# RWKV-7 time mixing: both Gram products of three key groups as one with 128 moved columns, receptances before the inverse, a new step order

## The chip, the core and the metric

One NeuronCore of a Trainium2 chip runs the kernel; the other cores of the chip are not used. The metric is the device time of one launch in microseconds (us). The engines have short names here as in the profile: PE is TensorE (matrix products; PEld is its loading of the stationary operand), DVE is VectorE, ACT is ScalarE, POOL is GpSimd, SP is SyncE, which issues the DMAs. PE writes into PSUM, which has eight banks of 128 x 512 float32; DVE and ACT read it.

## What is computed

A decoder trunk of two layers on 256 tokens of width 1024, in float32. The change lies wholly in the time mixing of the first layer, a delta rule with data-dependent decay over 16 heads of 64:

```python
r = xr @ w_rkv[0]; k = xk @ w_rkv[1]; v = xv @ w_rkv[2]
...
def step(S, inp):
    r_t, w_t, k_t, v_t, kk_t, b_t = inp
    sa = jnp.einsum('bhij,bhj->bhi', S, -kk_t)
    S = (S * w_t[:, :, None, :] + sa[..., None] * b_t[:, :, None, :]
         + v_t[..., None] * k_t[:, :, None, :])
    y = jnp.einsum('bhij,bhj->bhi', S, r_t)
    return S, y
...
_, y = lax.scan(step, S0, xs)          # 256 steps
# group norm per head, a bonus term, a gate, then
return (y * g) @ w_o
```

Around it stand the four gated FFNs (width 2816), the RMS norms and, in the second layer, sliding-window attention.

## The kernel before

The scan over 256 tokens is not run step by step. The tokens are cut into chunks of 64, and within a chunk the rule is solved as a triangular system: strictly causal 64x64 **Gram products** of the removal keys (`kk`) with the scaled keys and `b` vectors give the matrices `GS` and `GX`; a 32x32 **inverse** of their diagonal blocks runs on DVE (`invert`, step `inv`), `merge` (steps `m0`, `m1`) joins two 32x32 blocks to a 64x64 inverse `W`; a **chain** (`c00`, `c01` for the first pair of chunks of all heads, `c10`, `c11` for the second; the last digit is one half of the heads) multiplies with `GS`, `W`, `GX` in turn and copies between them on ACT; `state` (`st`) carries the state from the first pair to the second; `rows` (`y0`, `y1`) multiplies the causal Gram products with the **receptances** (`GR`, `GY`) to the output, and group norm (`gn0`, `gn1`), gate, transposition (`yt`) and output projection (`o0`, `o1`) follow.

Features go through in four **groups** p = 0 to 3 of 256 features (4 heads). For each group `k_mm` (`k0` to `k3`) projects the keys, `k_norm` (`n`) normalises and scales them, `r_mm` (`r`) projects the receptance, `r_fin` (`f`) scales it into AR and multiplies it with the key, `r_bo` (`b`) sums that for the bonus. `AR` holds four slots of 64 columns per head chunk: 0 and 3 are the removal keys of two chunks, 1 and 2 the receptances of the same two. Then, for each group, `g_pair` runs twice: as `s` with the removal keys (slots 0 and 3, strict mask, into GS and GX) and as `g` with the receptances (slots 1 and 2, inclusive mask, into GR and GY). One `g_pair` is 16 products with a stationary operand of 64 rows x 128 columns and 64 moved columns (line 681), two DVE evacuations with mask of 128x512 (line 684), eight more such products (line 692) and two ACT copies (line 695). The two products of a pair of heads use rows 0 to 63 and rows 64 to 127 of the array in turn (`hh`). A float32 product is recorded as two instructions, so 16 products stand as x32.

PSUM in this stage: four banks `bk` (tag of `self.bank()`), two `bc` (`self.cbank()`), two `bt` (`self.tbank()`), each in rotation.

What comes when is written out by hand: every step is a Python generator, and the string `STEPS` lists which generator goes on next. After that the order on PE, DVE and ACT is tied to the order in which the instructions were made:

```python
for nm in STEPS.split():
    next(unit[nm], None)
self.mark()
self.in_order(first, "PE", "DVE", "Activation")
```

So an instruction that waits holds up all that follows on its engine within this stage. `kw` splits the key weights (ACT, then DVE), `v01`, `v10`, `v11` project the values, `t0`, `t1` transpose keys, `w0` to `w7` split the output weights, `da` and `db` copy diagonal blocks of GS for the inverse, `bias` and `gate` prepare the group norm. Weights arrive through four rotating buffers `wr` from SP's queue. Outside this stage the kernel is the same.

Of the kernel before, what the change touches and what calls it, by code (L numbers as in the profile page):

```python
# [11 lines left out]
ALU = mybir.AluOpType  # L12
# [4 lines left out]
P = 128  # L17
# [5 lines left out]
N = 64  # L23
# [23 lines left out]
P3 = [(False, 0, 0)] * 3 + [(False, x, 2) for x in (-4, -4, -4, -3, -3, -1, -1)]  # L47
TX1, TX2 = (6, 7), (6, 7)
STEPS = """
kw kw kw k0 k0 kw k0 k0 kw kw xr k1 k1 xr kw xr xr n0 n0 kw kw n0 n0 r0 k1 k1  # L50
x1 kw kw n0 n0 k2 k2 n1 n1 n0 n1 n1 r0 f0 s0 kw s0 n1 n1 v01 k2 k2 kw kw k3 s1
s1 kw kw n2 x1 v01 n2 n2 n2 v01 k3 k3 f0 s0 n1 k3 n2 n2 n3 r3 n3 n3 s0 n3 s2 s2
v01 s1 n3 n3 r3 f3 n3 f3 s1 v01 room s3 s3 v10 v10 n2 b0 da r1 r1 db b0 t1 v10 v11 t0
v00 t0 t1 inv v10 s2 dc s2 inv v11 v11 t1 t1 t0 t0 inv r2 r2 f1 b3 s3 v11 inv s3 v10 inv
v11 inv g1 inv inv inv b3 m0 m0 c01 m1 m1 f1 b1 b1 g1 c00 m1 f2 w3 f2 m1 w0 w0 c01 g0
g0 b2 b2 w4 gate gate0 bias0 w4 bias0 c00 w3 gate0 gate0 m0 bias1 c01 m0 c01 gate0 g1 g1 c00 c00 g0 g0 c00
c00 c01 c00 c01 c10 c01 c01 c11 g2 g2 c00 st w1 g3 st g3 c11 w2 g3 g3 c10 w2 g2 g2 y0 c11
y0 w1 c10 c10 c10 bias1 c11 gn0 c10 gn0 c11 gn0 gn0 gn0 gn0 gn0 gn0 gn0 c11 c10 gate1 gate1 c11 gate1 w5 gn0
y1 w6 y1 c10 gn0 gn0 yt0 c10 gate1 w6 c11 w5 yt0 yt0 c11 y1 gn1 gn1 yt0 yt0 gn1 gn1 o0 o0 yt0 gn1
gn1 gn1 gn1 gn1 gn1 gn1 w7 o0 o0 o0 gn1 w7 o0 o0 yt1 yt1 yt1 yt1 o0 o1 o1 yt1 yt1 o1 o1 o1  # L60
o1 o1 o1
"""


class Trunk:
# [507 lines left out]
    def tm_core(self):  # L573
        nc, a, DC = self.nc, self.a, self.DC
        mm = nc.tensor.matmul
        TT, STT = nc.vector.tensor_tensor, nc.vector.scalar_tensor_tensor
# [6 lines left out]
        for j in range(2):  # L583
            t = self.pp.tile([P, D], F32, name=f"gain{self.uid()}", tag="gain", bufs=3)
# [36 lines left out]
        kw = lambda tag, shape, bufs: self.pools["kw"].tile(shape, F32R, name=f"{tag}_{self.uid()}", tag=tag, bufs=bufs)  # L621
# [10 lines left out]
        BH = self.tl("el", [P, 2, KT, P], tag="BH")  # L632
        Di = pk("Di", [P, KT, 4, N])
        AR = self.tl("ar", [P, 16, 4, N], tag="AR")
        BK = self.tl("ar", [P, 16, 4, N], tag="BK")
        nc.gpsimd.memset(Dp[:, :, :, 0], 1.0)
        sw, av = [], []
        for i in range(2):
            sw.append(pk("p1", [P, D], 2))
            for n in range(2):  # L640
                ns = slice(n * 512, n * 512 + 512)
                b = self.bank()
                mm(b, self.hwa[0:65, 0, toks[i]], l2[0][0:65, ns], start=True, stop=True)
                nc.scalar.activation(sw[i][:, ns], b, AF.Sigmoid)
        for p in range(4):
            b = self.bank()
# [6 lines left out]
        for n in range(2):  # L653
            for i in range(2):
                b = self.bank()
# [11 lines left out]
        masks = self.cst[:, K_MASK:K_MASK + 256].rearrange("p (e s t) -> p e s t", e=2, s=2)  # L667
        f = lambda ap: ap.rearrange("p s t -> p (s t)")
        GS = [self.tl("GS", [P, 16, 2, N], tag=f"GS{hh}") for hh in range(2)]
        GS = [(GS[hh], self.tl("GS", [P, 16, N], tag=f"GX{hh}")) for hh in range(2)]  # L670

        pair = lambda: [self.tbank() for _ in range(2)]

        def g_pair(p, lhs_rhs, dst, mask):
            bb = pair()
            for x in range(4):
                for sl in range(2):
                    for hh in range(2):
                        s = slice(hh * 64, hh * 64 + 64)
                        l, r = lhs_rhs(s, 4 * p + x, sl)  # L680
                        mm(bb[hh][:, (2 * x + sl) * N:(2 * x + sl + 1) * N], l, r, start=True, stop=True)  # L681
            yield
            for hh in range(2):
                TT(dst()[hh][0][:, 4 * p:4 * p + 4, :, :], bb[hh].rearrange("p (q s t) -> p q s t", q=4, s=2),
                   mask.unsqueeze(1).unsqueeze(1).to_broadcast([P, 4, 2, N]), op=ALU.mult)
            yield
            bb = pair()
            for x in range(4):
                for hh in range(2):
                    s = slice(hh * 64, hh * 64 + 64)  # L690
                    l, r = lhs_rhs(s, 4 * p + x, 2)
                    mm(bb[hh][:, x * N:(x + 1) * N], l, r, start=True, stop=True)  # L692
            yield
            for hh in range(2):
                nc.scalar.copy(dst()[hh][1][:, 4 * p:4 * p + 4, :], bb[hh][:, 0:256].rearrange("p (q t) -> p q t", q=4))
            yield

        def g_ops(slots):
            def at(s, q, sl):
                l = (lambda: f(BK[s, q, 0:2, :]), lambda: f(BK[s, q, 2:4, :]), lambda: BH[s, q % 2, q // 2, :])[sl]()  # L700
                return l, AR[s, q, slots[1] if sl else slots[0], :]
            return at

        kst = {}
        L = {}

        def k_split():
            for x in range(16):
                if x % 2 == 0:
                    raw = self.raw(a["w_k"][x // 2])  # L710
                w = kw("wk", [P, 2, 512], 3)
                ns = slice(x % 2 * 512, x % 2 * 512 + 512)
                self.split(w[:, 0], w[:, 1], raw[:, ns])
                kst["w", x] = w
                yield
# [63 lines left out]
        def r_mm(p):  # L779
            kst[p], todo = self.feat_raw(a["w_r"], p, L["xr"])  # L780
            for x in todo:
                x()
                yield
# [23 lines left out]
        def mix_xr():  # L807
            L["xr"] = self.tl("xt", [P, KT, T], tag="xth")
            for k in range(KT):
                self.mix_into(nc.vector, L["xr"][:, k], 0, k, slice(0, T))  # L810
                if k % 2:
                    yield

        def mix_xv1():
            L["xv1"] = vv[:, 1, :].rearrange("p (k t) -> p k t", k=KT)
            for k in range(KT):
                self.mix_into(nc.vector, L["xv1"][:, k], 3, k, toks[1])
                if k % 4 == 3:
                    yield

        def v_mm(i, n):
            acc, todo = v_half(n, L["xv1"] if i else xv)
            for x in todo:
                x()
                yield
            src = acc.rearrange("p (m hh j) -> p hh m j", hh=2, j=N)
            for e in range(2):
                rs = slice(e * 64, e * 64 + 64)
                dst = uv()[e].rearrange("p (hh m c) j -> p hh m c j", hh=2, c=2)[rs, :, n * 4:n * 4 + 4, i, :]
                nc.scalar.copy(dst, src[rs])  # L830
            yield

        def v00():
            src = v0.rearrange("p (m hh j) -> p hh m j", hh=2, j=N)
            for e in range(2):
                rs = slice(e * 64, e * 64 + 64)
                dst = uv()[e].rearrange("p (hh m c) j -> p hh m c j", hh=2, c=2)[rs, :, 0:4, 0, :]
                nc.scalar.copy(dst, src[rs])
            yield
# [9 lines left out]
        def room():  # L849
            self.close("kw", "pk")  # L850
            self.open("GR")
            self.open("Wx")
            self.open("el1")
            L["GR"] = [(self.tl("GR", [P, 16, 2, N], tag=f"GR{hh}"), self.tl("GR", [P, 16, N], tag=f"GY{hh}"))
                       for hh in range(2)]
            L["Dg"] = sp("c", [P, 32, 32])
            yield

        def dg(q0, q1):
            for x, (s0, sl, c0) in enumerate(((64, 0, 0), (96, 0, 32), (0, 1, 0), (32, 1, 32))):  # L860
                for hh in range(2):
                    (nc.vector.tensor_copy if q0 and hh else nc.scalar.copy)(
                        L["Dg"][s0:s0 + 32, hh * 16 + q0:hh * 16 + q1, :], GS[hh][0][s0:s0 + 32, q0:q1, sl, c0:c0 + 32])
            yield
# [33 lines left out]
        def decays():  # L898
            nc.scalar.copy(DC, Dp[:, :, :, N])
            yield  # L900
# [216 lines left out]
        def out_proj(i):  # L1117
# [3 lines left out]
            for k in range(KT):  # L1121
# [5 lines left out]

        unit = {"xr": mix_xr(), "x1": mix_xv1(), "room": room(), "da": dg(0, 12), "db": dg(12, 16), "inv": invert(),
                "dc": decays(), "kw": k_split(), "v00": v00(), "v01": v_mm(0, 1), "v10": v_mm(1, 0), "v11": v_mm(1, 1),
                "st": state(), "gate": gates()}  # L1130
        for p in range(4):
            unit.update({f"k{p}": k_mm(p), f"n{p}": k_norm(p), f"r{p}": r_mm(p), f"f{p}": r_fin(p), f"b{p}": r_bo(p),
                         f"s{p}": g_pair(p, g_ops((0, 3)), lambda: GS, masks[:, 0, 0]),
                         f"g{p}": g_pair(p, g_ops((1, 2)), GRs, masks[:, 0, 1])})
        for i in range(2):
            unit.update({f"m{i}": merge(i), f"t{i}": bk_turn(i), f"y{i}": rows(i), f"bias{i}": gn_bias(i),
                         f"gate{i}": gn_gate(i), f"gn{i}": normed(i), f"yt{i}": turned(i), f"o{i}": out_proj(i),
                         f"c{i}0": chain(i, 0), f"c{i}1": chain(i, 1)})
# [316 lines left out]
```

## Time and profile before

| | |
|---|---|
| median of 3 runs | 1082.4 us (1079.42 to 1084.34) |
| the profiled execution | 1087.76 us, of which the span of its instructions is 1086.0 us |
| PE busy, share of the span | 97% |
| DVE, ACT busy | 64%, 52% |
| DMA, mean | 169 GB/s |
| the stage of the change | from 235.0 us (first key product) to 418.0 us (end of the output projection) |

The profiled execution is one more run of the same kernel, 5.4 us above the median of the others. Busy time of PE includes the latency of products that overlap, so a busy PE can still run slowly: the granted clock says how fast it ran.

### The profile page before, as it was taken

Reading aid. Unit: us, or ns where it says so; the run is one execution under the profiler, and the core shown is the slowest. Engines: PE = TensorE matmul, PEld = TensorE weight load, DVE = VectorE, ACT = ScalarE, POOL = GpSimd, SP = SyncE. Lnnn points to the kernel's source line nnn. Section 1 sums busy time; section 2 is a strip of 40 time slices with the busy share of each in tenths; the row PEclk is TensorE's granted clock in tenths of the full one; section 3 lists DMA queues with packets and bytes.
Section 4 is the critical chain, followed back from the end, with each engine's and each line's share of the span. In section 5 each row is a group of like instructions: output and inputs, shape, how many; then the busy total and the mean of one; then the engine's idle time right before and its main releaser. Section 6 shows DMA issues by size and latency. Waiting matters only on the chain.

```text
span 1086.0 us, 16426 instructions
## 1 busy us (share of the span) xinstructions
PE 1058.1 (97%) x6408; PEld 878.3 (81%) x6408; DVE 693.2 (64%) x1108; ACT 566.4 (52%) x1014; POOL 32.7 (3%) x44
## 2 busy tenths in 40 slices
PE   7999999999999999999999999999999899999997
PEld 5888888698778987888888788888887568888885
DVE  6766654647696498855655686565656767665652
ACT  6654644464415346655554765555636665655541
POOL 0000000000000000000000100000012200000000
PEclk9999999999996899999999999999999999999999
DMA  8768664224363134866664286676532535765621
GB/s 290 237 193 290 197 191 136 74 101 137 123 187 95 45 118 156 272 202 207 191 193 137 97 271 204 188 249 194 180 110 98 175 97 195 214 211 187 184 76 39
DMA packets 52670, 183.06 MB, mean 169 GB/s; under 512 B 5744, under 2 KB 6000, under 8 KB 52464
## 3 DMA queue, kind: packets, MB, share of 16 engines
q1 hardware_dynamic: 52304, 181.49, 52.3%
q8 instruction: 50, 0.82, 0.3%
q10 hardware_dynamic: 288, 0.52, 0.1%
q14 instruction: 28, 0.23, 0.1%
HBM read 180.94 MB, written 1.05 MB: 168 GB/s over the span
## 4 chain that ended last, share of the span: by engine, by line
PE 90%; ACT 3%; DVE 2%; DMA 2%; issue 2%; POOL 1%; SPq 0%; DVEq 0%; POOLq 0%; ACTq 0%
PE bk L213 35%; PE bt L348 13%; PE bk L348 13%; PE bt L349 6%; PE bk L349 6%; PE bk L557 3%; PE bk L603 2%; PE bt L681 2%; PE bk L567 1%; PE bt L692 1%; PE bc L962 1%; PE bk L1013 1%; PE bt L295 1%; DMA wr<-in_w_in_dram 1%; ACT g2k L1236 1%
## 5 line engine op out<-in xcount | busy, mean ns | idle before, releaser
L187 DVE TENSOR_TENSOR W<-wr,W 128x1024 fp32r<-128x1024 f32 x275 | 335.8, 1226 | 192.7 <-ACT W L181 191.3
L181 ACT CAST W<-wr 128x1024 fp32r<-128x1024 f32 x280 | 292.8, 1051 | 200.8 <-issue 107.5
L213 PE MATMUL bk<-W,g2k 128*128 128x512 f32 x1056 | 251.5, 394 | 0.0
L213 PEld LDWEIGHTS bk<-W,g2k 128*128 128x128 f32 x1056 | 195.5, 188 | 45.1
L348 PE MATMUL bt<-xtl,W 128*128 128x512 f32 x296 | 105.9, 397 | 0.3 <-DVE xtl L336 0.3
L348 PE MATMUL bt<-xth,W 128*128 128x512 f32 x296 | 105.9, 396 | 0.0
L348 PE MATMUL bk<-xtl,W 128*128 128x512 f32 x296 | 105.7, 396 | 0.0
L348 PE MATMUL bk<-xth,W 128*128 128x512 f32 x296 | 105.7, 396 | 0.0
L349 PE MATMUL bt<-xtl,W 128*128 128x256 f32 x296 | 83.1, 281 | 0.0
L349 PE MATMUL bk<-xth,W 128*128 128x256 f32 x296 | 83.1, 281 | 0.0
L349 PE MATMUL bt<-xth,W 128*128 128x256 f32 x296 | 83.1, 281 | 0.0
L349 PE MATMUL bk<-xtl,W 128*128 128x256 f32 x296 | 83.0, 280 | 0.0
L348 PEld LDWEIGHTS bt<-xtl,W 128*128 128x128 f32 x296 | 55.6, 188 | 14.0 <-DVE xtl L336 0.7
L348 PEld LDWEIGHTS bk<-xth,W 128*128 128x128 f32 x296 | 55.6, 188 | 13.3
L348 PEld LDWEIGHTS bt<-xth,W 128*128 128x128 f32 x296 | 55.5, 188 | 13.3
L348 PEld LDWEIGHTS bk<-xtl,W 128*128 128x128 f32 x296 | 55.6, 188 | 13.0
L213 PE MATMUL bk<-W,xtl 128*128 128x512 f32 x216 | 55.9, 404 | 1.5 <-ACT xtl L300 0.7
L349 PEld LDWEIGHTS bk<-xtl,W 128*128 128x128 f32 x296 | 55.8, 188 | 1.3
L349 PEld LDWEIGHTS bt<-xtl,W 128*128 128x128 f32 x296 | 55.8, 189 | 0.1
L349 PEld LDWEIGHTS bk<-xth,W 128*128 128x128 f32 x296 | 55.8, 189 | 0.0
L349 PEld LDWEIGHTS bt<-xth,W 128*128 128x128 f32 x296 | 55.7, 189 | 0.1
L213 PE MATMUL bk<-W,xth 128*128 128x512 f32 x216 | 53.5, 394 | 0.0
(260 smaller groups left out, 1429.0 us busy)
## 6 DMA issues: line engine op xcount, KB each, us to landing
wr<-in_w_in_dram SPq DMA_DIRECT2D x148, 512.0 KB, 4.0
wr<-in_w_out_dram SPq DMA_DIRECT2D x88, 512.0 KB, 3.6
wr<-in_w_in_lead_dram SPq DMA_DIRECT2D x28, 512.0 KB, 4.0
wr<-in_w_v_dram SPq DMA_DIRECT2D x16, 512.0 KB, 3.7
gain<-in_rows_dram SPq DMA_DIRECT2D x13, 512.0 KB, 4.6
wr<-in_w_k_dram SPq DMA_DIRECT2D x8, 512.0 KB, 4.2
wr<-in_w_r_dram SPq DMA_DIRECT2D x8, 512.0 KB, 4.2
wr<-in_w_o_dram SPq DMA_DIRECT2D x8, 512.0 KB, 3.8
```

What stands on the lines that cost most here:

```text
L181: self.follow(nc.scalar.copy(w[:, 0, :], raw), 0)
L187: self.follow(nc.vector.tensor_tensor(w[:, 1, :], raw, w[:, 0, :], op=ALU.subtract), 1)
L213: mm = lambda *x, **y: self.nc.tensor.matmul(*x, **y, **kw)
L295: t = self.nc.tensor.transpose(b[:, k * P:(k + 1) * P], xn[:, c:c + P], self.ident)
L348: mm(banks[j], hi[:, c0:c0 + P], xt[c][:, :, k4, :], start=(k == 0), stop=False)
L349: use[0] = mm(banks[j][:, 0:T], lo[:, c0:c0 + P], xt[c][:, 0, k4, :], start=False, stop=(k == KT - 1))
L557: self.nc.tensor.matmul(b[:, j * T:(j + 1) * T], ws[k // 4][:, c0:c0 + P], xf[:, k, :], start=(k == 0), stop=(k == KT - 1))
L567: nc.tensor.matmul(bs[j], l[:, k, j * P:(j + 1) * P], x[:, k, sl], start=(k == 0 and not e), stop=(k == KT - 1 and e == 1))
L603: mm(acc, x[:, 2 * k2 + k, :], w[:, k, :], start=(k2 + k == 0), stop=(k2 + k == 4))
L681: mm(bb[hh][:, (2 * x + sl) * N:(2 * x + sl + 1) * N], l, r, start=True, stop=True)
L692: mm(bb[hh][:, x * N:(x + 1) * N], l, r, start=True, stop=True)
L962: mm(b[r, m * N:(m + 1) * N], W[r, v - hh * 16, :], XV[r, v, :], start=True, stop=True)
```

## The change

A new generator `g_both(p)` makes the products of `s` and `g` of one group together: for each stationary operand the two neighbouring slots of AR (a removal key and a receptance) are moved at once, 128 columns in place of 64. It has three parts of eight products each, in a pair of `bk`, `bt` and `bc` banks; the first two are evacuated by four DVE instructions of 128x256 each (the half for GS with the strict mask, the half for GR; both read the mask of their kind), the third by four ACT copies of 128x256. Groups 0, 1 and 2 use it (steps `q0`, `q1`, `q2`); group 3 keeps `s3` and `g3`. Since a `q` needs the receptances of its group, `r0`, `r1`, `r2` now come before the inverse, and `STEPS` is written anew from end to end; `r3` and most of the value products stand within the inverse.

```diff
@@ STEPS (one line of each; the table is replaced whole)
-v11 inv g1 inv inv inv b3 m0 m0 c01 m1 m1 f1 b1 b1 g1 c00 m1 f2 w3 f2 m1 w0 w0 c01 g0
+g3 inv m1 c01 m1 m0 m0 g3 c00 m1 m1 f3 b3 b3 w0 gate0 bias0 bias0 c01 q2 q2 q2 c00 g3 gate0 gate0
...
+        def g_both(p):
+            for sl, new in enumerate((lambda: [self.bank() for _ in range(2)], pair,
+                                      lambda: [self.cbank() for _ in range(2)])):
+                bb = new()
+                for x in range(4):
+                    q = 4 * p + x
+                    for hh in range(2):
+                        s = slice(hh * 64, hh * 64 + 64)
+                        l = BH[s, q % 2, q // 2, :] if sl == 2 else f(BK[s, q, 2 * sl:2 * sl + 2, :])
+                        mm(bb[hh][:, x * P:(x + 1) * P], l, f(AR[s, q, 2 * min(sl, 1):2 * min(sl, 1) + 2, :]),
+                           start=True, stop=True)
+                yield
+                qs = slice(4 * p, 4 * p + 4)
+                for kind in range(2):
+                    for hh in range(2):
+                        G = (GS, L["GR"])[kind][hh]
+                        b = bb[hh].rearrange("p (q s t) -> p q s t", q=4, s=2)[:, :, kind if sl == 0 else 1 - kind, :]
+                        if sl == 2:
+                            nc.scalar.copy(G[1][:, qs, :], b)
+                        else:
+                            TT(G[0][:, qs, sl, :], b, masks[:, 0, kind].unsqueeze(1).to_broadcast([P, 4, N]),
+                               op=ALU.mult)
+                    yield
...
+        for p in (0, 1, 2):
+            unit[f"q{p}"] = g_both(p)
```

Where the new order tells most, in rows of the two programs as they are built (line, operation, output and inputs, shape; lines behind `g_both` are 24 to 26 higher in the changed kernel).

DVE, just ahead of the inverse, before: GS is the masked Gram product, `c` the diagonal blocks, `a` and `b` the inverse's matrices.

```order
L792 SCALAR_TENSOR_TENSOR km_1938<-bk_2468,cols,km_1938 128x256 x2
L684 TENSOR_TENSOR GS_316_2006<-bt_2571,cst 128x512
L684 TENSOR_TENSOR GS_317_2007<-bt_2572,cst 128x512
L774 TENSOR_TENSOR BH_1939<-BK_1942,Dp_1937 128x2x2x128
L862 COPY c_2570<-GS_317_2007 32x128 x4
L875 STREAM_TRANSPOSE a_2668<-c_2570 128x1024
L880 TENSOR_TENSOR c_2673<-a_2668,b_2669 128x31
```

The same place in the changed kernel (L727 is `g_both`'s evacuation, L886, L798 and L899 are the old L862, L774 and L875):

```order
L727 TENSOR_TENSOR GR_382_2481<-bk_2585,cst 128x4x64
L727 TENSOR_TENSOR GR_384_2483<-bk_2586,cst 128x4x64
L727 TENSOR_TENSOR GS_316_2006<-bt_2609,cst 128x4x64
L727 TENSOR_TENSOR GS_317_2007<-bt_2610,cst 128x4x64
L727 TENSOR_TENSOR GR_382_2481<-bt_2609,cst 128x4x64
L727 TENSOR_TENSOR GR_384_2483<-bt_2610,cst 128x4x64
L886 COPY c_2485<-GS_317_2007 32x128 x4
L798 TENSOR_TENSOR BH_1939<-BK_1942,Dp_1937 128x2x2x128
L899 STREAM_TRANSPOSE a_2678<-c_2485 128x1024
```

The last evacuations ahead of the inverse are now those of `q2`, and 24 of them stand in a row from `s3` on, where before two of `s3` stood.

PE, after the merges, before: L1049 is the gate, L916 the second half of a merge, L962 a chain's product with W, L692 a part of `g1`.

```order
L802 MATMUL bc_3063<-cst,km_1938 128x2 x4
L1049 MATMUL bk_3081<-wr_3073,sgT 128x512
L1049 MATMUL bk_3093<-wr_3073,sgT 128x512
L916 MATMUL bc_3095<-a_2870,b_2874 32x32 x32
L962 MATMUL bc_3133<-xtl_2915,W_467_2873 64x64 x8
L692 MATMUL bt_3147<-AR_1941,BH_1939 128x64
```

And now (L1073, L940, L986, L976 and L1037 are the old L1049, L916, L962, L952 and L1013):

```order
L1073 MATMUL bk_3103<-wr_2884,sgT 128x512
L986 MATMUL bc_3110<-xtl_2950,W_478_2911 64x64 x8
L940 MATMUL bc_3120<-a_2878,b_2912 32x32 x32
L976 MATMUL bk_2951<-u_2817,GX_319_2009 64x64 x8
L986 MATMUL bc_3164<-xtl_2950,W_477_2910 64x64 x8
L986 MATMUL bc_3174<-xtl_2950,W_478_2911 64x64 x8
L976 MATMUL bk_3007<-u_2817,GX_318_2008 64x64 x8
L1073 MATMUL bk_3197<-wr_2884,sgT 128x512
L986 MATMUL bc_3212<-xtl_2950,W_477_2910 64x64 x8
L1037 MATMUL bk_3222<-u_2817,GR_382_2481 64x64
```

The parts of `g0` and `g1` that stood between the chain's products are gone, the gate's four products are spread among them, and `y0` (L1037) follows straight on.

DVE, around the state between the two pairs of chunks, before: L992 and L993 scale the new state, L684 is `g2` and `g3`.

```order
L684 TENSOR_TENSOR GR_395_2566<-bt_3252,cst 128x512
L684 TENSOR_TENSOR GR_397_2568<-bt_3253,cst 128x512
L992 TENSOR_TENSOR c_3273<-bc_3274,DC 128x512
L993 TENSOR_TENSOR c_3273<-c_3273,DC 128x512
L684 TENSOR_TENSOR GR_395_2566<-bt_3311,cst 128x512
```

And now (L1016 and L1017 are the old L992 and L993; L1105 to L1118 are the group norm of the first half, L1075 and L1076 its gate):

```order
L1105 TENSOR_REDUCE gst_3272<-bk_3223 128x8
L1106 TENSOR_SCALAR gst_3272<-gst_3272 128x8
L1107 TENSOR_TENSOR xth_2891<-bk_3223,gst_3272 128x8x64
L1075 TENSOR_TENSOR gain_2886<-gain_2886,bk_3285 128x512
L1076 TENSOR_TENSOR gain_2888<-gain_2888,bk_3285 128x512
L1113 TENSOR_REDUCE gst_3272<-b_3273 128x8
L1114 TENSOR_SCALAR gst_3272<-gst_3272 128x8
L1118 TENSOR_TENSOR xth_2891<-xth_2891,gain_2890 128x8x64
L1016 TENSOR_TENSOR c_3323<-bc_3324,DC 128x512
L1017 TENSOR_TENSOR c_3323<-c_3323,DC 128x512
```

The state's two instructions now stand behind most of the first half's group norm, which itself waits for `y0`.

## Rows read from the trace of the kernel before

**Rows 1.** The profile's page: busy time of PE and DVE, and the line of the granted TensorE clock in 40 slices of the span (27.15 us each; 9 is full speed, 5 would be half).

```profile
PE 1058.1 (97%) x6408; PEld 878.3 (81%) x6408; DVE 693.2 (64%) x1108; ACT 566.4 (52%) x1014; POOL 32.7 (3%) x44
...
PEclk9999999999996899999999999999999999999999
```

**Rows 2.** The sums by stretch over the stage: length, busy time (and instructions) of PE, PEld, DVE, ACT and POOL, then the granted clock, the share of the DMA engines and GB/s.

```profile
235.00:297.80 62.80, 62.80 (x490) 54.14 (x489) 41.93 (x83) 31.08 (x66) 1.11 (x2) 1.00 0.39 127
297.80:330.30 32.50, 32.50 (x186) 23.92 (x185) 29.30 (x70) 7.94 (x18) 0.00 (x0) 1.00 0.61 182
330.30:335.90 5.60, 5.07 (x188) 4.79 (x188) 2.67 (x5) 3.40 (x9) 0.00 (x0) 1.00 0.20 78
335.90:360.30 24.40, 24.40 (x290) 20.98 (x284) 13.55 (x18) 9.44 (x17) 0.00 (x0) 0.51 0.20 66
360.30:373.50 13.20, 13.20 (x312) 12.63 (x312) 6.47 (x9) 4.18 (x7) 0.00 (x0) 1.00 0.02 5
373.50:376.90 3.40, 3.40 (x54) 3.28 (x54) 0.89 (x1) 1.71 (x4) 0.00 (x0) 0.50 0.80 288
```

**Rows 3.** The chain of work that ended last, in order of time (start, length, what): a pass of the 16 Gram products and one of the eight at full clock, 32 receptance instructions of 256 moved columns (one group's `r`), two of the four parts of a value product, and two turns of keys (`t`).

```profile
292.86 1.93 PE bt L681 x32
...
299.21 7.01 PE bk L557 x32
...
306.66 3.44 PE bk L603 x8
...
312.25 1.04 PE bt L692 x16
...
316.92 0.87 PE bt L974 x8
```

**Rows 4.** PE in order of time in the attention stage (start, length of the group, line, shape of the stationary operand, what is written): products of 64 rows x 128 columns with 128 moved columns, four on one half of the rows and then four on the other half, and what starts next.

```profile
823.55 2.82 PE L1222 MATMUL bk<-kT,qT 64*128 64x128 f32 x32 [0.19 <-DVE qT L1199]
826.29 0.73 PE L213 MATMUL bk<-W,xtl 128*128 128x512 f32 x2
```

**Rows 5.** DVE in order of time: evacuations from PSUM of two widths, the copy of diagonal blocks, the start and the end of the inverse.

```profile
294.10 0.87 DVE L792 SCALAR_TENSOR_TENSOR km<-bk,cols,km 128x256 f32<-128x256 f32 x2
294.89 1.27 DVE L684 TENSOR_TENSOR GS<-bt,cst 128x512 f32<-128x512 f32 x2
296.08 0.68 DVE L774 TENSOR_TENSOR BH<-BK,Dp 128x512 f32<-128x512 f32 x1
296.80 0.92 DVE L862 COPY c<-GS 32x128 f32<-32x128 f32 x4
297.81 1.95 DVE L875 STREAM_TRANSPOSE a<-c 128x1024 f32<-128x1024 f32 x1
...
327.68 0.88 DVE L895 TENSOR_SCALAR W<-a,cst 128x512 f32<-128x512 f32 x2
```

**Rows 6.** The chain of work that ended last, from the end of the inverse on: the first half of a merge, twice (L907), the chain's first products (L937), a bonus sum (L802), and two pieces of the low-clock stretch.

```profile
330.37 1.13 PE bc L907 x64
331.50 1.08 PE bk L937 x32
332.58 1.00 PE bc L907 x56
334.43 0.98 PE bc L802 x8
335.41 1.46 PE bk L937 x32
...
338.71 3.61 PE bt L681 x32
...
357.18 3.22 PE bk L952 x32
```

**Rows 7.** The same view around the state (L988) and after it: the chain's product with the state (L945), `g3`'s first pass (L681), `y0` (L1013), two products with W (L962), two with GX (L952), two of the gate (L1049) and the state's part of `y1` (L1003).

```profile
365.68 2.06 PE bc L988 x64
367.74 1.93 PE bt L681 x32
369.67 1.08 PE bk L945 x32
...
374.88 4.80 PE bk L1013 x96
379.68 2.00 PE bc L962 x32
381.68 2.14 PE bk L952 x32
383.82 1.92 PE bk L1049 x4
385.74 1.84 PE bk L1003 x62
```

**Rows 8.** DVE in order of time: the state's two instructions, and the first instruction of each half of the heads in the group norm `gn0` (three instructions each).

```profile
367.78 0.69 DVE L992 TENSOR_TENSOR c<-bc,DC 128x512 f32<-128x512 f32 x1 [0.78 <-PE bc L988]
368.50 0.69 DVE L993 TENSOR_TENSOR c<-c,DC 128x512 f32<-128x512 f32 x1
...
378.78 0.69 DVE L1081 TENSOR_REDUCE gst<-bk 128x8 f32<-128x512 f32 x1 [4.39 <-PE bk L1013]
...
380.32 0.68 DVE L1081 TENSOR_REDUCE gst<-bk 128x8 f32<-128x512 f32 x1
```

More of the change, by code (lines that the diff above doesn't have):

```diff
@@ L49 @@
 STEPS = """
[L50 to L54, printed above, removed]
-v11 inv g1 inv inv inv b3 m0 m0 c01 m1 m1 f1 b1 b1 g1 c00 m1 f2 w3 f2 m1 w0 w0 c01 g0
[L56 to L61, printed above, removed]
+kw k0 kw k0 kw k0 kw kw k0 x1 xr kw k1 kw kw k1 k1 dc xr kw kw xr xr k1 k2 k2
+kw n0 n0 n0 r0 n0 kw kw n0 n0 n1 n1 x1 r0 f0 f0 k2 k2 n1 n1 k3 r1 kw kw kw n1
+n1 n2 n2 n2 n2 r1 f1 f1 n1 f1 n0 k3 k3 n2 n2 k3 n3 n3 b1 n3 r2 b1 n3 n3 n3 n3
+room r2 f2 f2 s3 s3 q1 q1 q1 q0 q1 q1 q1 q0 q0 b0 b2 b0 q0 q0 q0 b2 q2 q2 q2 q0
+q2 q2 v11 q2 db t1 v01 v01 da q0 v01 t0 v11 t1 q0 n2 inv v01 f2 inv t0 inv inv q1 q1 s3
+s3 q1 v10 inv inv v11 t0 v11 r3 v01 inv r3 t1 v10 v00 v11 f0 t1 v10 v10 t0 f3 v10 inv w0 gate
+g3 inv m1 c01 m1 m0 m0 g3 c00 m1 m1 f3 b3 b3 w0 gate0 bias0 bias0 c01 q2 q2 q2 c00 g3 gate0 gate0
+w5 w5 c01 c01 m0 m0 c01 c01 f1 c00 c00 c01 c01 c00 bias1 gate1 c00 w3 bias1 gate1 w3 gate0 g3 c00 c00 f0
+y0 y0 gn0 gn0 gn0 w4 gate1 c11 c10 gate1 st w2 gn0 gn0 gn0 gn0 st y1 c11 gn0 c10 c11 c11 gn0 gn0 gn0
+c10 c10 gn0 c11 w4 c11 w6 w6 c10 yt0 yt0 yt0 yt0 yt0 yt0 w1 w1 w2 c10 c10 c11 y1 c10 c10 c11 c11
+y1 gn1 gn1 gn1 gn1 gn1 f2 o0 gn1 o0 w7 gn1 gn1 gn1 o0 o0 o0 o0 gn1 gn1 gn1 o0 w7 yt1 yt1 o0
+yt1 o1 o1 yt1 yt1 yt1 o1 o1 o1 o1 o1 o1
 """
```

## Prediction, made before the changed kernel was run

> **What bounds the kernel now.** I read the page first: PE is busy 97% of the span, DVE 64%, and the granted clock is full everywhere except in the 13th and 14th slice [rows 1]. The sums by stretch put that dip inside the stage of the change: PE runs at 0.51 of its clock from 335.9 to 360.3 us and at 0.50 from 373.5 to 376.9 [rows 2], 27.8 us in all. In every stretch shown but one PE has no idle time; from 330.3 to 335.9 it is busy 5.07 of 5.60 us. The reader should see two things: PE's own list of products ends last, so work taken off it counts in full, and part of that work is paid for at nearly twice its price.
>
> What does the dip cost? The same 32 Gram instructions take 1.93 us at full clock [rows 3, 7] and 3.61 in the dip [rows 6], a ratio of 1.87. By it 27.8 us of low clock do the work of 14.9: the dip costs **12.9 us**. Ahead of its fall PE worked 5.5 us on narrow pieces: 32x32 merges, 64x64 chain products and a bonus sum with two moved columns [rows 6].
>
> **The change, part by part.**
>
> *Gram products.* `s` plus `g` of one group cost 2 x (1.93 + 1.04) = 5.94 us [rows 3]. A `q` has three parts of 16 instructions with the same stationary shape and 128 moved columns. Is a part as cheap as 16 instructions with 64 columns (1.04 us), or nearly twice as dear? The attention stage has this shape: 32 instructions start between 823.55 and 826.29, 86 ns each [rows 4]. Were streaming the bound and the two halves of the array's rows never at work together, the pace of the receptances (7.01 us for 32 of 256 columns, so 110 ns for 128 columns [rows 3]) would give 3.5 us for these 32; they took 2.74. So the halves do overlap, though there they change only every eight instructions, while `q` changes at each product. Bounds of a part: 1.04 us (full overlap) and 16 x 110 ns = 1.75 us (none); by the attention row as it stands, 16 x 86 ns = 1.37. I take 1.04: the 64-column pace, 60 to 65 ns for an instruction [rows 3], is 120 to 130 for a pair, one in each half, and that already leaves room for 110 ns of streaming in each. A `q` then costs 3.1 us, and three save 3 x 2.8 = **8.5 us**; at the other end 3 x (5.94 - 5.25) = 2.1 us. All of it lies on PE's list.
>
> The Trainium skill, "TensorE: Matmul & The Clock Gate" (section "Back-to-back issue gap"), gives a lone matmul 134 cycles for 128 moved columns against some 60 for up to 64, so that joining two narrow ones would gain nothing; by that page the sum would lack the 8.5 us.
>
> *Evacuations.* Each `q` has eight DVE instructions of 128x256 in place of four of 128x512. Two of 512 columns take 1.19 us from start to the next start, two of 256 columns 0.79 [rows 5]. So a `q` asks for 3.2 us of DVE against 2.4, and 24 instructions stand in a row right ahead of the inverse: 9.5 us, or 14.3 if 256 columns cost what 512 do. What hides them is PE, which has eight parts of `q` (8.3), `s3`, two bonus sums and a value product there, as much or more. I went down the lists of PE, ACT and DVE in the new order with the durations of the trace, from the first key product at 235.0 us, and get the last evacuation near 296.5, diagonal blocks (0.9) and one BH (0.6 [rows 5]) behind it, and the inverse beginning near 298, where it began before (297.81 [rows 5]).
>
> *What is moved ahead of the merges.* All four receptances stood ahead of the first merge before too, though within the inverse. PE's list up to it loses `s0` to `s2` and `g1`'s first pass (3 x 2.97 + 1.93 = 10.8) and gains eight parts of `q` (8.3), `g3`'s first pass (1.9) and one bonus sum (0.8): 11.0. So PE reaches the merge as before, near 330. The inverse is covered: behind `q2`'s second part stand twelve value parts (1.72 each), `r3` (7.0), four turns (0.44 each), two third parts (1.04 each) and `g3`'s first pass, 33.4 us [rows 3], against some 31 us from the inverse's start to its W [rows 5]. I count nothing; bounds: 1.5 us gained (what the old kernel waited ahead of the merge, by the sum of its list), 5 us lost (below).
>
> *ACT, DMA.* ACT has as many copies as before and 52% load [rows 1]: nothing. SP issues the same loads through four `wr` buffers, `w_r` earlier and `w_v` later; I find them filled 0 to 2 us ahead of use, `v10`'s last part perhaps 0.4 us late. Nothing, with 1 us as bound.
>
> *The state.* Before, `st` ended at 367.74 and its two DVE instructions ran at once, beside `g3`'s 1.93 us on PE [rows 7, 8]: no wait. Now they stand on DVE behind most of `gn0`, which can only start when `y0` ends. On PE a gate product (0.96), two first chain products (1.08 each [rows 6]) and `st` (2.06 [rows 7]) follow `y0`: 5.2 us. On DVE 2 x 1.54 (`gn0`'s halves [rows 8]), a gate of 1.2, some 0.4 of waiting for ACT, 0.8 and 0.6 of `gn0`'s second step and the state's 1.4 make 7.5. PE's next piece, `y1`, reads that state, and all of PE's list, the chain `c10` and `c11` first, is queued behind it. A new wait of 2 to 3 us; I take **2.4**; bounds 0 (if low clock stretches PE's side beyond DVE's) and 3.1.
>
> *The low clock.* Two places behind the inverse decide. (a) From the first merge to `y0`. The first 6.2 us at full clock are narrow pieces as before, without the 0.5 us of idling [rows 2, 6]; then come two gate products of 512 columns, `q2`'s last part and a part of `g3`, chain products again, and `y0`, 4.8 us over all 128 rows [rows 7]. The clock came back before when products over all rows (L952) had run for 3.2 us, and the second time while `y0` ran [rows 2, 6, 7]. If it falls after the narrow pieces again and returns in `y0`, twelve pieces of about 1.0 us [rows 7] are paid at 1.87: 10.4 lost. (b) From the new wait to `y1`'s product over all rows: 9 us of mostly narrow pieces, where the old order had `g3`, `g2` and `y0` among them: 0 to 7.8 lost. Together 0 to 18.2; both places hold pieces of either kind, so I take the middle, 9.1. Against 12.9 before, **3.8 us** come back.
>
> **Sum.** -8.5 - 3.8 + 2.4 = -9.9 us, 1087.8 -> 1077.9 for the profiled execution. That one lay 5.4 us above the median of the runs; from the median the sum gives **1072.5 us**. A difference under 0.5% (5.4 us) this measurement can hardly tell from none.
>
> **Rivals.**
>
> *Low clock as long as before* (13 us lost or a little more). For it: the same narrow pieces lead it in. Against it: the `g` passes that filled it are gone. -8.5 + 2.4 = -6.1: 1076.3, near the border of what can be told.
>
> *No low clock.* For it: gate and `q2` products follow sooner. Against it: the merges, 32x32 as ever, and the new wait. -8.5 - 12.9 + 2.4 = -19.0: 1063.4.
>
> *The halves do not overlap with 128 columns.* A part takes 1.75 us: -2.1 + 2.4, the clock as before: 1082.7. Against it stands the 86 ns row [rows 4]. The page of the Trainium skill named above for lone matmuls would come out here.
>
> *The evacuations bind* (the other side). If a 128x256 evacuation costs 0.60 us as a 128x512 one does, the 24 take 14.3 us, the inverse starts 5 us later, and PE, whose list ahead of the merges is hardly longer than DVE's, waits 5 us at the merge, right ahead of the narrow pieces; low clock then costs as much as before or up to 5 us more. -8.5 + 2.4 + 5.0 + 0 to 5: -1 to +4; with 3 us of late loads and waits for banks in the packed stretch +7: 1081 to 1089. It decides from an inverse start of about 303 us on. Against it: two 256-wide ones took 0.79 [rows 5]. The Trainium skill, "TensorEngine Tiling (Array Packing)" (section "Performance Considerations", "PSUM Bottleneck"), warns of this: packed products go faster, their evacuation does not, and the copy can become the bound.
>
> **Chances.** Forecast (low clock costs some two thirds of before): 0.43, 1067 to 1077. As long as before: 0.25, 1074 to 1080. None: 0.14, 1060 to 1066. No overlap: 0.06, 1080 to 1085. Evacuations bind: 0.12, 1081 to 1090. The range 1063 to 1081 leaves out most of the last and about half of "none" and of "no overlap". Faster (under 1077.0): 0.43 + half of 0.25 + 0.14 = 0.70. Slower (over 1087.8): half of the last case, 0.06. Same: 0.24. The likeliest case alone spans 1067 to 1077.
>
> **What the profile after would show.** Parts of `q` (L716): 16 instructions in about 1.0 us; 1.75 would be no overlap. The inverse's first transposition near 298 us and no wait of PE ahead of the first merge. PE idle 2 to 3 us behind the state's products, released by DVE's L1016 or L1017. A low clock of some 20 us in all. The output projection ending near 408 us instead of 418.0. I would be wrong above all if the low clock lasted through both places, or if small waits between 235 and 298 us, where I count no more than the old kernel had, add up and move the inverse.

## The result, and the profile after

The changed kernel took 1067.87 us (median of four executions, 1066.84 to 1068.75) against 1083.37 us of the kernel before (1079.42 to 1087.21): ratio 0.986, 95% interval 0.982 to 0.990. That is 15.5 us less, where I had forecast 9.9, and inside my range. The profiled execution took 1066.84 us, its span is 1065.0 us; before it was 1087.76 and 1086.0. Three executions taken for the experiments (1098.3 and 1307.6 us of the kernel before, 1165.3 us of a variant) were in a slower state and are left out of every comparison here.

The page of the changed kernel, the lines that answer [rows 1]:

```profile
PE 1037.6 (97%) x6264; PEld 860.1 (81%) x6264; DVE 694.0 (65%) x1120; ACT 566.5 (53%) x1014; POOL 36.0 (3%) x44
...
PEclk9999999999999999999999999999999999999999
```

PE has 144 instructions fewer, as nine parts of 16 in place of 32 must give, and 20.5 us less busy time. The clock line has no dip at all. The sums by stretch answer [rows 2] (columns as there):

```profile
236.30:299.90 63.60, 63.60 (x517) 58.90 (x516) 48.27 (x105) 29.38 (x65) 1.11 (x2) 1.00 0.35 109
299.90:330.30 30.40, 30.40 (x151) 18.69 (x149) 28.17 (x69) 10.19 (x23) 0.00 (x0) 1.00 0.71 225
330.30:397.40 67.10, 66.23 (x1126) 57.08 (x1123) 54.23 (x85) 36.43 (x67) 2.18 (x2) 1.00 0.35 116
```

This execution began the stage at 236.3 us, 1.25 later than the one before, so stretches are compared by length. From the first key product to the first merge: 94.06 us, before 95.26. From there to the end of the output projection: 67.1, before 87.7, of which 27.8 at half clock. What follows differs by 0.4 us.

The chain of work that ended last, ahead of the inverse (L716 is a part of `q`, L826 the bonus sums), and behind the merges. It answers [rows 3, 6, 7]:

```profile
286.55 1.93 PE bt L681 x32
288.48 1.84 PE bk L716 x32
290.32 0.89 PE bt L716 x16
291.21 1.88 PE bc L826 x16
293.09 1.09 PE bt L716 x16
294.18 0.89 PE bk L716 x16
295.07 0.89 PE bc L716 x16
295.97 0.93 PE bt L716 x16
...
332.63 1.09 PE bc L931 x61
333.72 0.09 issue
...
338.21 1.09 PE bc L716 x16
...
349.50 3.88 PE bk L1037 x96
...
356.45 2.08 PE bc L1012 x64
358.53 0.02 issue
358.55 0.70 DVE c L1016
359.25 0.04 issue
359.30 1.85 PE bk L1027 x60
```

A part of `q` costs 0.89 to 1.09 us; eight of the nine stand here and the ninth, within the inverse, took 1.09. Beside 0.09 us in the second merge the only wait of PE behind the merges is the one for the state's first scaling (L1016): 0.77 us from 358.53 to 359.30.

DVE in order of time, the last evacuations, the diagonal blocks and the start of the inverse, for [rows 5]:

```profile
296.89 0.75 DVE L727 TENSOR_TENSOR GS<-bt,cst 128x256 f32<-128x256 f32 x2
297.56 0.74 DVE L727 TENSOR_TENSOR GR<-bt,cst 128x256 f32<-128x256 f32 x2
298.34 0.91 DVE L886 COPY c<-GS 32x128 f32<-32x128 f32 x4
...
299.89 1.99 DVE L899 STREAM_TRANSPOSE a<-c 128x1024 f32<-128x1024 f32 x1
```

Two evacuations of 256 columns take 0.67 us from start to the next start.

### The profile page after: what moved, and what is told of

Read it like the earlier page. It is cut to its first block, busy times and chain, and to the rows that moved or that the text cites. A ratio compares the mean times of both kernels' runs of the same rounds, so it can differ in the third digit from the quotient of the medians.

```text
span 1065.0 us, 16153 instructions
## 1 busy us (share of the span) xinstructions
PE 1037.6 (97%) x6264; PEld 860.1 (81%) x6264; DVE 694.0 (65%) x1120; ACT 566.5 (53%) x1014; POOL 36.0 (3%) x44
## 4 chain that ended last, share of the span: by engine, by line
PE 90%; DVE 3%; DMA 2%; issue 2%; ACT 2%; POOL 1%; SPq 0%; POOLq 0%; DVEq 0%; ACTq 0%
PE bk L213 36%; PE bt L348 13%; PE bk L348 13%; PE bt L349 7%; PE bk L349 7%; PE bk L557 3%; PE bk L603 2%; PE bk L567 1%; DMA wr<-in_w_in_dram 1%; PE bc L986 1%; PE bk L1037 1%; PE bt L295 1%; PE bk L1286 1%; DVE t L245 1%; ACT W L181 1%
```

## The experiments

**How far does one execution speak for the kernel?** Both kernels once more, unchanged.

> The kernel before once more, unchanged. Its 25 executions of the first comparison lie between 1078.4 us at a mean granted clock of 0.999 and 1098.3 us at 0.976, so how long its clock is low differs from one execution to the next. Theory A (the low clock of the profiled execution covered waits of PE that the old order has at full clock, so it cost less than the 12.9 us that I counted): an execution with a clock of 0.995 or more shows PE waiting some 2 to 4 us in all behind the merges, and from the first merge to the end of the output projection 77 to 79 us. Theory B (the 12.9 us are right): no more waits than before, and 75 us there at full clock.

Measured: 1084.8 us (median of ten), and in the profiled execution a quite different low clock. The sums by stretch from its first merge to the end of the output projection:

```profile
333.20:344.10 10.90, 10.02 (x307) 9.39 (x306) 3.69 (x6) 7.24 (x15) 0.00 (x0) 1.00 0.11 41
344.10:347.50 3.40, 3.40 (x25) 1.24 (x25) 3.39 (x7) 1.43 (x2) 0.00 (x0) 0.50 0.53 154
347.50:368.00 20.50, 20.50 (x464) 19.58 (x458) 15.75 (x21) 8.37 (x16) 0.00 (x0) 1.00 0.22 58
368.00:371.40 3.40, 3.40 (x59) 3.28 (x58) 0.58 (x1) 1.71 (x4) 0.00 (x0) 0.50 0.81 282
371.40:412.30 40.90, 40.90 (x426) 34.49 (x423) 34.52 (x59) 18.67 (x35) 1.10 (x2) 1.00 0.33 105
```

The same instructions in the same order, and 6.8 us at half here instead of 27.8. Over the 59 executions of this kernel that were taken for the experiments the mean granted clock lies between 0.980 and 0.999 and the time between 1091.1 and 1077.8 us: about 0.73 us for each 0.001 (a fit). Their median is 1083.1 us at 0.991; the nine at 0.998 or more have a median of 1078.7. So low clock costs this kernel 4.4 us in the median execution, and by my price nearly three times as much in the one that I had profiled (which lay 9.1 us above 1078.7).

The stage is not the only place. The clock line of this execution has its one dip in the 32nd slice:

```profile
PEclk9999999999999999999999999999999899999999
```

There, in the attention of the second layer (818.4 to 822.0 and 845.8 to 852.8 us), PE ran at half clock for some 10 us, where the first profile shows full clock. Three of the variants below have 7 to 10 us of it there too (the moved gate product, the wide products, the changed kernel with the bonus sums moved), in code that the change doesn't touch. So the 4.4 us hold for the whole program; how much of them lies in the stage, no run here shows.

Neither theory was right as put. PE does wait in this execution (0.88 us from 333.2 to 344.1, mostly in the second merge), which theory A asked for, but less than its 2 to 4 us. The stretch takes 79.1 us; less 6.8 x 0.465 = 3.2 it is 75.9 at full clock, against 87.7 - 12.9 = 74.8 in the first profile. So my price for the low clock (1 - 1/1.87 = 0.465 us for each us of it) holds to about a us.

> The changed kernel once more, unchanged, for the spread of its executions. Theory A (the new order keeps the clock up whatever the execution): mean granted clock 0.995 to 0.999 in nearly every execution, and times within 1066 to 1070 us. Theory B (the four executions so far were lucky): a share of them as low as 0.985 to 0.99, up to 1075 us.

Measured: 1067.4 us, four executions from 1066.7 to 1068.1 at 0.995 to 0.999; ratio 0.985 (0.983 to 0.986). Theory A. All eight of the changed kernel lie within 2.0 us, median 1067.6.

**The joining alone undone**, the order of the steps kept.

> The changed kernel with the joining alone undone: each product of q with 128 moved columns is made as two of 64, same stationary operand, same banks, same evacuations, same order of steps. A part of q then has 32 instructions. Theory A (joining pays through the instructions it saves, and the order of the steps, not the joining, keeps the clock up): a part goes from 0.95 to about 1.93 us, the nine parts add 8.5 to 9 us, the granted clock stays full through the stage: about 1076.6 us. Theory B (the joined products are what keeps the clock full): the low clock comes back behind the merges, 8.5 us and some 10 us of low clock on top: about 1086 us.

```diff
-mm(bb[hh][:, x * P:(x + 1) * P], l, f(AR[s, q, 2 * min(sl, 1):2 * min(sl, 1) + 2, :]), start=True, stop=True)
+for j in range(2):
+    c = x * P + j * N
+    mm(bb[hh][:, c:c + N], l, AR[s, q, 2 * min(sl, 1) + j, :], start=True, stop=True)
```

Measured: 1083.1 us, ratio to the kernel before 1.002 (0.998 to 1.005). The chain ahead of the inverse, and the sums by stretch:

```profile
287.81 3.62 PE bk L718 x64
291.44 1.79 PE bt L718 x32
293.22 1.88 PE bc L827 x16
295.10 2.09 PE bt L718 x32
297.19 3.42 PE bk L718 x32
```
```profile
287.80:296.80 9.00, 9.00 (x145) 8.92 (x143) 5.45 (x14) 1.51 (x6) 0.00 (x0) 1.00 0.15 55
296.80:310.50 13.70, 13.70 (x106) 11.85 (x104) 5.87 (x18) 4.33 (x10) 0.00 (x0) 0.50 0.01 1
```

A part takes 1.8 us at full clock, about 0.88 more than joined: 9 x 0.88 = 7.9 us, a little under theory A's sum. The clock falls too, theory B's claim, but at a place that I had not named: ahead of the inverse, in the run of Gram products, while PE has no idle time. 13.7 x 0.465 = 6.4. Together 14.3 of the 15.5 us to the 1067.6 of the changed kernel. The mean clock says that this execution is no exception: it lies between 0.975 and 0.992 in all ten, against 0.995 to 0.999 in the eight of the changed kernel. The order without the joining thus brings nothing that can be measured in the median.

**Is it the bonus sums?** In that run two of them stood 1.8 us ahead of the fall. Here they stand within the inverse, with 64 moved columns and with 128.

> The kernel with 64 moved columns once more (each joined product made as two), with the two bonus sums b0 and b2, 16 instructions of two moved columns in 1.88 us, taken out of the run of Gram products ahead of the inverse and put behind six parts of value products within it. In the run with 64 columns the clock had fallen 1.8 us behind these sums. Theory A (the bonus sums, in which PE hardly moves a column, make the clock fall): the clock stays full ahead of the inverse, which gives back the 13.7 us at half, some 6 us: about 1077 us. Theory B (the long run of products with 64 moved columns does it by itself): it falls there as before, about 1083 us, or 1 to 2 us less since the run is shorter.

> The changed kernel with the same two bonus sums moved in the same way, so that PE has 1.9 us less to do between the Gram products ahead of the inverse, where DVE is busy 13.1 of 14 us with evacuations, and 1.9 us more within the inverse. Theory A (DVE's evacuations are already the bound there, and the bonus sums are cover): PE waits 1 to 1.9 us for banks, the inverse starts no earlier, the merge comes 1 to 1.9 us later: 1068.4 to 1069.5 us, and 3 to 4 us more if the clock falls in that wait. Theory B (there is cover left): no change, 1067.6 us.

```diff
-... q0 q0 b0 b2 b0 q0 q0 q0 b2 q2 q2 q2 q0 ... t0 v11 t1 q0 n2 inv ...
+... q0 q0 q0 q0 q0 q2 q2 q2 q0 ... t0 v11 t1 q0 b0 b2 b0 b2 n2 inv ...
```

Measured with 64 columns: 1085.1 us (ratio 1.004, 1.001 to 1.007), and the clock falls in the same run without the bonus sums, for longer:

```profile
287.50:295.10 7.60, 6.38 (x112) 6.27 (x111) 4.86 (x13) 1.18 (x4) 0.00 (x0) 1.00 0.18 63
295.10:312.10 17.00, 17.00 (x127) 14.71 (x126) 8.12 (x20) 4.52 (x10) 0.00 (x0) 0.50 0.00 1
```

Theory B. But the two runs differ in one more thing: with the bonus sums gone PE waits 1.22 us for a bank about a us ahead of the fall. The other run tells the two apart. With 128 columns PE waits there as well, and the clock stays full, here and to the end of the stage. PE in order of time, the first part behind the wait, and the sums of that run:

```profile
292.43 1.35 PE L716 MATMUL bt<-AR,BK 64*128 64x128 f32 x15 [1.26 <-DVE GR L727]
```
```profile
288.20:296.50 8.30, 7.04 (x118) 6.72 (x115) 7.92 (x22) 2.05 (x6) 0.00 (x0) 1.00 0.18 60
```

So of the four combinations both with 64 columns fell and both with 128 held. The mean clocks of all executions go the same way: at most 0.992 in the twenty with 64 columns, at least 0.993 in the twelve with 128 (the 0.993 is the profiled execution, whose low clock lies in the attention). For the second question this run asks theory A holds: DVE is busy 7.92 of 8.30 us and is the bound, the merge comes 1.5 us later behind the first key product (95.6 against 94.06 us), and the time is 1069.5 us, 1.9 more (four executions, 1067.1 to 1071.5). The bonus sums are cover.

**How near are the evacuations to binding?**

> The changed kernel with q1's eight evacuations on DVE made twice each (same values): 8 x 0.33 = 2.6 us more of DVE's list ahead of the inverse, nothing else changed. Theory A (DVE's list up to the end of the inverse and PE's list up to the first merge end nearly together, so that the evacuations are about to bind): the inverse starts 2 to 2.6 us later and PE waits 1.5 to 2.6 us at the first merge: 1069.5 to 1071 us, more if the clock falls in it. Theory B (there is cover left): the merge starts where it did, 1068 us.

```diff
-TT(G[0][:, qs, sl, :], b, masks[:, 0, kind]..., op=ALU.mult)
+for _ in range(2 if p == 1 else 1):
+    TT(G[0][:, qs, sl, :], b, masks[:, 0, kind]..., op=ALU.mult)
```

Measured: 1072.7 us, 5.1 more than the changed kernel. Theory A in its size and beyond, but at another place: PE waits for banks between the parts of `q`, not at the merge, and at the end of the wait the clock falls. The chain that ended last goes over DVE from 288.0 to 294.8 us; PE behind it, and the sums:

```profile
294.95 2.61 PE L716 MATMUL bt<-AR,BK 64*128 64x128 f32 x15 [2.38 <-DVE GR L728]
```
```profile
287.80:294.80 7.00, 4.76 (x68) 4.55 (x66) 6.58 (x17) 1.51 (x6) 0.00 (x0) 1.00 0.21 70
294.80:301.60 6.80, 6.63 (x56) 6.39 (x58) 5.02 (x14) 1.83 (x4) 0.00 (x0) 0.50 0.01 2
```

2.4 of waiting and 6.8 x 0.465 = 3.2 of low clock: 5.6. So joined products do not hold the clock in every case: over the wait of 1.26 us in the run before it stayed full, over this one of 2.4 it did not, in one profiled execution each.

**Do the halves of the array overlap only when products alternate?**

> The changed kernel with the products of a part of q in another order: the four on rows 0 to 63 first, then the four on rows 64 to 127, where they alternate otherwise. Theory A (the two halves of the array's rows work at once only when the products alternate between them): a part goes from 0.95 us to the 86 ns per instruction of the attention row, 1.37 us, or to 1.75 without any overlap: 3.8 to 7 us slower than the changed kernel, 1071.5 to 1075 us. Theory B (the pace is set by something else, issue for instance): no change, 1068 us.

```diff
-for x in range(4):
-    q = 4 * p + x
-    for hh in range(2):
+for hh in range(2):
+    for x in range(4):
+        q = 4 * p + x
```

Measured: 1072.1 us. Three parts stand between the first two starts of the chain, and the value products follow at the third:

```profile
288.19 2.27 PE bk L716 x29
...
291.90 1.88 PE bc L826 x16
...
298.74 1.49 PE bk L603 x3
```

3.71 us for three, 1.24 each, 77 ns for an instruction, where the changed kernel has 0.91 (288.48 to 291.21). Theory A, a little cheaper than the 86 ns of [rows 4], where the side changes just as often. But in `q` each half writes a bank of its own, so that this edit also takes away the change of bank and of the half that gets the next stationary operand; the run doesn't tell which of them counts. Nine parts at 0.33 more are 3.0 us. The profiled execution (1070.6 us) lies 3.7 above that of the changed kernel, and PE waits 0.8 us more in its second merge; the other 0.7 us of the median I did not place.

This run also answers a rival for the clock. Joined, the run of Gram products is simply shorter: in the changed kernel it lasts 8.4 us from the first part of `q` (288.48) until products of 512 columns follow (296.90), and with 64 columns the clock fell 9.0 and 7.5 us behind the first part. Here the run lasts 10.6 us (288.19 to 298.74), longer than both, and the clock stays full through the stage (one profiled execution; the mean clocks of the four are 0.992 to 0.999). So the length of the run alone does not make the clock fall.

**More narrow work behind the merges.**

> The changed kernel with more narrow work: the bonus sum of group 3, which stands right behind the merges, is made five times instead of once (the same sums, 2 moved columns each), so that PE has 32 more of these instructions there. Theory A (a run of narrow pieces behind the merges, with nothing wide among them, is what lets the clock fall): 0.91 x 4 = 3.6 us of work, and the granted clock falls to half right there, for 5 to 20 us that cost 2.5 to 10 more: 1074 to 1081 us. Theory B (narrow pieces alone do not matter, something else made the old order fall): 3.6 us, clock full: about 1071.5 us.

```diff
-for i in range(2):
+for i in list(range(2)) * (5 if p == 3 else 1):
     for j in range(2):
         mm(bo[:, h:h + 2], prod[:, j, toks[i]], HI, ...)
```

Measured: 1076.0 us, ratio to the kernel before 0.997 (0.994 to 1.000). The bonus sums run from 337.9 us on:

```profile
337.90:340.50 2.60, 2.60 (x28) 2.60 (x24) 0.00 (x0) 1.15 (x2) 0.00 (x0) 1.00 0.07 25
340.50:347.30 6.80, 6.80 (x32) 5.29 (x34) 2.83 (x5) 0.74 (x2) 0.00 (x0) 0.50 0.01 2
```

Theory A, in the profiled execution: the clock falls within them, for 6.8 us, and comes back when the gate's 512-column products and the joined `q2` follow. 3.6 + 3.2 us, and 0.5 more of waiting in the second merge; 8.4 were measured.

**Wide products among the narrow ones of the old order.**

> The kernel before with four idle-purpose products of 512 moved columns over all 128 rows added on PE (results unused), one behind each of the first chain product, the second merge, the bonus sum and the second chain product after the inverse; everything else as before. They add 4 x 1.03 = 4.1 us of work. Theory A (the first low-clock stretch comes from the run of narrow pieces): the stretch of 23.9 us that began at 335.96 us is gone or mostly gone, which gives back up to 11 us: 7 us faster than before in all, about 1076 us. Theory B (the clock falls for another reason): 4 us slower than before, about 1087 us, with the same dip.

```diff
+def wide():
+    for _ in range(4):
+        mm(self.tbank(), self.sgT[:, 0:P], self.cst[:, K_MASK:K_MASK + 512], start=True, stop=True)
+        yield
-... m0 m0 c01 m1 m1 f1 b1 b1 g1 c00 m1 ...
+... m0 m0 c01 dm m1 dm m1 f1 b1 dm b1 g1 c00 dm m1 ...
```

Measured: 1084.0 us, ratio 1.002 (1.000 to 1.004). The whole stretch behind the merges, one row:

```profile
331.60:412.00 80.40, 79.39 (x1268) 67.48 (x1267) 57.98 (x91) 37.53 (x71) 1.10 (x2) 1.00 0.29 92
```

The mechanism of theory A is there: no low clock in the stage, and a median of the mean clocks of 0.996 against 0.991, though single executions of the kernel before have 0.999 without such products. Its sum is not: the median execution had at most 4.4 us of low clock to give, not 11, and the four products cost 4.1. The row also gives the old order's stretch at full clock: 80.4 - 4.1 = 76.3 us.

**Work into the new wait.**

> The changed kernel with one gate product moved: the one behind y0 goes behind the state's products, its evacuation on DVE behind the state's two instructions. It is work for PE while it waits for the state's scaling, and it takes 1.2 us out of DVE's list ahead of that. Theory A (the 0.79 us that PE waits ahead of y1 can be filled): the wait is gone and y1 starts some 0.8 us earlier behind y0 than now: 1067 us, which the time can hardly show but the trace can. Theory B (another wait takes its place): no gain.

```diff
-y0 y0 gn0 gn0 gn0 w4 gate1 c11 c10 gate1 st w2 gn0 gn0 gn0 gn0 st y1
+y0 y0 gn0 gn0 gn0 w4 c11 c10 st gate1 w2 gn0 gn0 gn0 gn0 st gate1 y1
```

Measured: 1069.9 us, 2.3 more. Theory B: `y1` starts behind the gate at 363.36 and stops after two instructions: what goes on waits for L1076, the evacuation of the moved gate product, whose bank it needs. PE in order of time:

```profile
363.36 0.33 PE L1027 MATMUL bk<-c,AR 64*64 64x64 f32 x2
365.07 1.84 PE L1027 MATMUL bk<-c,AR 64*64 64x64 f32 x60 [1.39 <-DVE gain L1076]
```

The 0.8 us of waiting became 1.4, which is 0.6 of the 2.3 us; the rest I did not place. In its profiled execution (1074.3 us) the clock was also low from 334.3 to 344.5 us, right behind a wait of 1.0 us in the second merge, where its order is still that of the changed kernel (whose profile has 0.09 us there): the new order makes the fall rarer, not impossible.

No run here beats the changed kernel.

## Why the prediction was right, and where its steps failed

*Gram products: right.* 1.04 us for a part, 0.89 to 1.09 measured; `s` and `g` of three groups cost 17.8 us [rows 3], the nine parts 8.7, so 9.1 saved where I had 8.5. The choice between the bounds was right, and the reason given is borne out as far as the runs go: with alternating halves 16 instructions keep the pace of the 64-column ones, and when the alternation (of halves and of banks) is taken away the pace of the attention row nearly comes back. The figures of the Trainium skill for a lone matmul ("TensorE: Matmul & The Clock Gate", "Back-to-back issue gap"), by which joining gains nothing, fit this stream by half: the 134 cycles for 128 columns, an estimate of 56 ns at 2.4 GHz or 0.9 us for a part, against 56 to 68 ns here; but not the some 60 cycles for up to 64 columns, 25 ns, against 56 to 65 ns here. The same row of that table names a floor of some 62 ns for each matmul as the other case, which is near; whether it sets the pace here, no run shows.

*Evacuations: right in the sum, thin in the margin.* 0.39 us (read from L792, another instruction of that width) was 0.34; the inverse starts 63.6 us behind the first key product, 63.0 forecast. No wait at the first merge. But "as much or more" of cover on PE was close: without 1.9 us of bonus sums, or with 2.6 us more of DVE, the rival of binding evacuations appears, as a wait for banks. It is the rule of the Trainium skill, "TensorEngine Tiling (Array Packing)" ("PSUM Bottleneck"), met at its edge: 1.9 and 5.1 us in these two runs (of the 5.1 some 3.2 are low clock), none in the changed kernel.

*Ahead of the merge: 0 forecast, 1.2 gained,* most of my upper bound of 1.5: the eight parts of `q` there took 7.6 us where I had 8.3, which is 0.7 of it. The rest I did not place: by [rows 2] PE had no idle time there before.

*The state: mechanism right, size wrong.* 2.4 forecast, 0.77 measured. Two lines of DVE show why:

```profile
352.49 0.69 DVE L1105 TENSOR_REDUCE gst<-bk 128x8 f32<-128x512 f32 x1 [0.40 <-PE bk L1037]
...
358.55 0.69 DVE L1016 TENSOR_TENSOR c<-bc,DC 128x512 f32<-128x512 f32 x1 [0.33 <-PE bc L1012]
```

Three terms of DVE's 7.5 us failed. `gn0` starts at the first finished bank of `y0`, 0.9 us ahead of its end at 353.38; the 0.4 us of waiting for ACT did not come; and PE needs L1016 alone, not L1017, 0.7 less. That leaves 5.5 us, and 5.5 were measured: 4.8 until DVE was free at 358.22, and 0.7 for L1016. `st` ended a little later, at 358.53, so that the wait is only that of one scaling behind `st`. (`y0` itself took 3.88 us; its 4.8 in [rows 7] had been measured partly at half clock.)

*The low clock: the failed step.* I charged the median with what one execution had lost. The forecast subtracted 3.8 us on the grounds that the new order would lose 9.1 of 12.9. In the profiled executions all 12.9 came back, the "no low clock" rival, to which I gave 0.14. In the medians at most some 4.4 were there to come back. Both errors have one source: [rows 2] show one execution. What I gave as the reason, that two stretches of narrow pieces would decide, points the right way (the runs with more narrow work and with 64 columns fell, the one with wide products did not). But I had not seen that the joining itself keeps the clock up: the run without it fell ahead of the inverse, where I had counted no low clock at all.

The sum by medians: 15.5 us between 1083.1 and 1067.6. Of these 4.4 are low clock, in the stage or in the attention. The other 11.1 lie between 1078.7 and 1067.6, at nearly full clock: 1.2 ahead of the merge; 8 to 9 behind it (75 to 76 us at full clock against 67.1: of the `g` passes of 9.95 us by [rows 3] 1.9 remain, the new wait adds 0.8, and short waits such as the 0.9 us in the old second merge go); 1 to 2 us stay unplaced. The forecast of 9.9 had the same parts, with a wait 1.6 us too large, waits of the old kernel left out, and a low clock that was right in size only by chance.

## What to carry to other kernels

Where a stationary operand serves two narrow products, try to move both at once: here, with alternating row halves and banks, 128 columns took PE no longer than 64 (0.91 us for 16 instructions against 0.9 to 1.04). Count what it asks of the engine that evacuates, and of the banks. A low clock seen in one profile is a property of that execution: take its cost from the times and mean clocks of many, look where in the program it lies, and compare kernels at equal clock first. A piece of work that is moved to fill a wait takes a PSUM bank with it: look up who holds the bank that the next product needs.

## What the runs showed of the hardware that I had not expected

The granted clock fell while PE was busy without a gap. In the run with 64 columns PE was busy 9.00 of 9.00 us before the fall at 296.8, and 13.70 of 13.70 in it; what it did there were packed products of 64 rows with few moved columns. The same operands through half as many instructions with twice the columns kept full clock, 2.4 GHz, also where their run took 10.6 us without a gap (with the halves grouped). And the fall is not fixed by the program: the kernel before had 27.8 us of it in the stage in one execution and 6.8 in another, which had 10 more in the attention. Why one execution falls and another doesn't, these runs do not settle.
